# A trunk of an SSD layer and a stick-breaking attention layer: the order of an MLP's last sums, of the first units' projection steps and of the output projection's end

## The chip, the cores and the metric

The kernel runs on one core of one Trainium2 chip. The metric is the device time of one execution in microseconds (us). The kernel before takes 1426.51 us in the median of three runs, from 1426.31 to 1427.24.

The core has five engines with a queue of instructions each. TensorE (PE) multiplies matrices, VectorE (DVE) and ScalarE (ACT) work element by element, GpSimd (POOL) does the small rest, and SyncE (SP) issues the transfers (DMA) of weights. An engine executes its own queue in order. An instruction that waits for another engine holds up all that is queued behind it.

## The reference

A sequence of 512 tokens with 1024 features passes two layers, each of a mixer and an MLP. Each of the four parts ends in `h = LayerNorm(alpha * h + part(h))`. Cut to what the change touches:

```python
# layer 0: Mamba-2 mixer, then
h = layer_norm(ALPHA * h + square(relu(h @ w1)) @ w2)     # first MLP, w1: 1024 x 4096
k, v = h @ w_k, h @ w_v                                   # 16 heads of 64
# layer 1: stick-breaking attention
q = (h @ w_q) * 64 ** -0.5
for each block of 128 queries, key blocks from the diagonal one backwards:
    z = q @ k.T                      # masked: only keys s < t
    # w[t, s] = sigmoid(z[t, s]) * prod over s < j < t of (1 - sigmoid(z[t, j]))
    o += w @ v
h = layer_norm(ALPHA * h + o @ w_o)                       # output projection
h = layer_norm(ALPHA * h + square(relu(h @ w1)) @ w2)     # second MLP
```

## The kernel before

**Numbers in two halves.** Every fp32 operand of a matmul is split into a high part `hi` (rounded to the type fp32r) and a low part `lo`, which is what rounding left out. A product takes three matmuls, hi·hi, hi·lo and lo·hi (`mm3`, lines 207 to 209 of the profile). The high part is a cast on ScalarE (line 190 for weights, 398 for activations), the low part a subtraction on VectorE (192 and 399; every fourth weight tile's on GpSimd in some stretches).

**Weights.** All weight tiles stand in one list, `stream`, in the order in which they are used. `emit_w` fetches the next one by DMA into a raw tile of 128x1024 (line 166), casts it (190) and subtracts (192). `prefetch(n)` does so until n tiles are ready beyond those taken, and `load_w` takes one tile and prefetches some ahead. What is called where in the program decides where a fetch, a cast and a split stand in the queues of SyncE, ScalarE and VectorE. Tiles are numbered along the list: `wr153` is the raw tile, `wh153` and `wl153` its halves. A few tiles go into other buffers (`alt`): `wvp` in the space of the attention's v weights, `wq` and `wk` in that of its q and k weights.

**Order.** A scheduler puts each engine's instructions in order by its own estimate of when they can start, within what the program's order and dependences allow. `tc.issue_after(x)` holds the instructions under it behind instruction x on x's engine; it adds no wait for another engine.

**End of the first MLP.** The second matrix product of an MLP is done in a form with fewer products: seven named ones (P1 to P7) accumulate in banks X, Y, Z and V of PSUM, and `add` (line 431 where the row sums for the norm are taken along) adds a bank to v, the running sum with the residual. A tile of v has four row blocks of 128 tokens. They are normed in pairs, 0 and 1 first, then 2 and 3. `Norm` takes row sums (342), squares (345 on ScalarE), a power on GpSimd (347 to 353), shifts (358) and scales (364) on VectorE; `turn` transposes the normed rows on TensorE (395) and splits them into `ln1_hh` and `ln1_hl` (398, 399), the input of all projections behind. In the last quarter of the first MLP the last two products (P2 into bank V, P3 into Y), their sums and the second pair's norm are all held behind the first pair's norm by one `issue_after`.

**Attention.** The v, q and k projections of head pair 0 (`pv`, `pq`, `pk`) come first. Then a software pipeline runs over 48 units: head pair m (0 to 7), head hd (0, 1), block of queries and keys b (0 to 2). At step s, `z_stage` (lines 1077 to 1096) computes the logits z of unit s and its log terms `sp` (halves `sp..h`, `sp..l`, by ScalarE's Exp and Ln and VectorE's max); `w_stage` (1119 to 1127) of unit s-2 adds the sums over keys on TensorE and takes the exponent, `w..h` and `w..l`; `pv_stage` (1139 to 1153) of unit s-3 multiplies with v into `o`, and after a head's last unit evacuates it (1147 to 1153). A unit is named by its three digits: `w710h` is the high part of w for head pair 7, head 1, block 0. Between the stages `fill.run(step)` puts projection steps of the next head pairs as filler (three matmuls each), 16 or 24 of them over 18 calls. In the last units the output projection's first column half is the filler (`ao`, `ao_early`, `w_o`), as far as head pairs 0 to 5 go.

**Output projection's end and the second MLP's start.** `ao_late` finishes the projection (banks `al`, first digit the column half n, second the row block): for rows 0 and 1 and then rows 2 and 3, what is left of column half 0 (head pairs 6 and 7) and all of half 1, then adds them to v (1040, 1042), takes statistics (1043) and norms. The transposes of rows 0 and 1 stand among the products of rows 2 and 3. `mlp_first` then multiplies the normed rows by the first four weight tiles (bank `f`); two of these tiles are fetched ahead by `ao_late`.

Of the kernel before, what the change touches and what calls it, by code (L numbers as in the profile page):

```python
# [14 lines left out]
ALU = mybir.AluOpType  # L15
PSUM = bass.MemoryType.PSUM

P = 128
T = 512
# [10 lines left out]
ALPHA = (2 * 2) ** 0.25  # L30
# [5 lines left out]
def trunk(ctx: ExitStack, tc: tile.TileContext, io):  # L36
    nc = tc.nc
# [7 lines left out]
    def psum(tag, shape, name):  # L45
        return ps.tile(shape, F32, tag=tag, name=name, bufs=4)
# [32 lines left out]
    ntri_ge = cp.tile([P, P], F32R, name="ntri_ge")  # L79
# [4 lines left out]
    stream = []  # L84
    marks = []
# [13 lines left out]
    def w1_tile(layer, i):  # L99
        return io["w1"][layer, 8 * (i // 8) + M_ORDER[i % 8]]  # L100
# [30 lines left out]
    for m in range(KD - 1):  # L131
        stream += [io["w_qk"][m + 1, j] for j in range(2)]
        if m in v_at:
            stream += [io["w_v"][v_at.index(m) + 1, j] for j in range(2)]
    alt_o = len(stream) + 3
    stream += [io["w_o"][0, i] for i in range(4)] + [w1_tile(1, 0)]
    stream += [io["w_o"][1, i] for i in range(4)] + [w1_tile(1, 1)]
    marks.append(len(stream))
    mlp_stream(1)
    del stream[marks[2]:marks[2] + 2]  # L140
# [1 line left out]
    ready = []  # L142
    taken = [0]
    extra = [None, 0, 0, True, 0]
    alt = {}
    sums = {}
    depth = [2]

# [73 lines left out]
    class Filler:  # L222
# [4 lines left out]
        def add(self, gen):  # L227
            self.queue.append(gen)
# [172 lines left out]
    PAIRS = [(0, 1), (2, 3)]  # L401
# [11 lines left out]
    def mlp(layer, ln, nxt, pts):  # L413
# [5 lines left out]
        with tc.tile_pool(name=f"mlp{layer}", bufs=1, reuse_waits="tile") as mp:  # L419
# [3 lines left out]
            def add(row, n, pts, stats=False, js=(0, 1)):  # L423
                for j in js:
                    t = rows[row][j]
                    vs = v[:, t, n * T:(n + 1) * T]
                    if (t, n) not in started:
                        started.add((t, n))
                        nc.vector.scalar_tensor_tensor(vs, vs, ALPHA, pts[j], ALU.mult, ALU.add)
                    elif stats:  # L430
                        nc.vector.scalar_tensor_tensor(vs, vs, 1.0, pts[j], ALU.mult, ALU.add,
                                                       accum_out=nxt.sm[:, t, n:n + 1])
                    else:
                        nc.vector.tensor_add(vs, pts[j], vs)

            for q in range(4):
                last = q == 3
# [509 lines left out]
    def attention(ln, nxt):  # L947
# [4 lines left out]
        with tc.tile_pool(name="att", bufs=2, reuse_waits="tile") as at:  # L952
# [16 lines left out]
            def qk_w(i):  # L969
                return tuple(at.tile([P, 1024], F32R, tag=n + "2", name=f"w{n}{i}", bufs=2) for n in "qk")  # L970
# [54 lines left out]
            def ao(*args):  # L1025
                for _ in ao_steps(*args):
                    pass
# [8 lines left out]
            def ao_evac(pts, n, tt):  # L1036
                for j, t in enumerate(tt):
# [61 lines left out]
            def w_stage(u):  # L1099
                m, hd, b = u  # L1100
                nm = f"{m}{hd}{b}"
                z, s = st[u]
                n = z.shape[1]
                sa, sb = st[m, hd, 0][1], st[m, hd, min(b, 1)][1]
                off = 0
                for j in blocks[b]:
                    zj = z[:, off:off + qn[j]]
                    own = [x[:, off:off + qn[j]] for x in s]
                    off += qn[j]
                    terms = []  # L1110
                    if j == 2:
                        terms = [(P, [x[:, 2 * P:3 * P] for x in sa])]
                    elif j < 2:
                        terms = [((2 - j) * P, [x.rearrange("p (a c) -> p a c", c=P)[:, 0::3, :] for x in sa])]
                    if j == 0:
                        terms.append((P, sb))
                    for c0, tt in terms:
                        for x in tt:
                            nc.tensor.matmul(zj[:, c0:], none_r, x, start=False, stop=False, skip_group_check=True)
                    for i, x in enumerate(own):  # L1120
                        nc.tensor.matmul(zj, ntri_ge, x, start=False, stop=i == 1, skip_group_check=True)
# [4 lines left out]
                nc.scalar.activation(ws[0], z, AF.Exp)  # L1126
                nc.vector.tensor_sub(ws[1], w, f(ws[0]))
                st[u] = (z, s, ws)
# [36 lines left out]
            w_o, wv_of, w_1, pin = {}, {}, [], [None]  # L1165
# [16 lines left out]
            for s in range(len(units) + 3):  # L1182
                if s < len(units):
# [96 lines left out]
```

## Time and profile before

| what | value |
|---|---|
| median of three runs | 1426.51 us (1426.31 to 1427.24) |
| profiled execution | 1426.79 us |
| span of the profiled execution | 1424.7 us, 19323 instructions |
| matmuls | 7414 |
| DMA | 162.99 MB, 114 GB/s in the mean |

The span runs from the first to the last instruction that the profile shows; 2.1 us of the profiled execution lie around it. The busy share of an engine is a mean over stages with different limits. So a stage is read by itself: in a timeline each row is a start, a duration, the engine, the line, the operation, out<-in, and in brackets how long the engine sat idle before the row and which engine's result ended that wait. PEclk is the clock granted to TensorE, 1.00 being full speed. The chain of waits follows the work that ended last, step by step.

### The profile page before, as it was taken

How to read it: one execution, taken by the hardware profiler on the slowest of the kernel's cores; microseconds unless marked ns; L12 is line 12 of the kernel's file. 1: busy time of each engine (PE TensorE's matmuls, PEld its weight loads, DVE VectorE, ACT ScalarE, POOL GpSimd, SP SyncE). 2: the span in 40 equal slices, each digit the busy share in tenths (PEclk: the TensorE clock that was granted, in tenths of full speed). 3: DMA queues.
4: the chain of work that ended last, by engine and by line, in shares of the span. 5: the costliest groups of instructions: out<-in, count | busy, mean ns of one | idle time of the engine just before them, and what ended most of it. 6: DMA issues, size and time to landing. Idle time of an engine off the chain costs nothing. (4 is left out here: it accounts for less than half of the span.)

```text
span 1424.7 us, 19323 instructions
## 1 busy us (share of the span) xinstructions
PE 1394.1 (98%) x7414; PEld 1199.9 (84%) x7414; DVE 1078.2 (76%) x1530; ACT 783.9 (55%) x1264; POOL 221.4 (16%) x249
## 2 busy tenths in 40 slices
PE   9999999999999999999999899999999999999996
PEld 6898897889997988888888789899878888888885
DVE  5798898368877695876849868787867876858587
ACT  5556574246653453626345468898842735454453
POOL 2344555135443100000000200000000000000001
PEclk9999999999999999999999999999999999999999
DMA  5223212221223356455443421121223455454533
GB/s 185 75 77 131 75 60 75 89 89 60 75 75 104 125 157 179 132 179 161 148 148 120 146 89 38 52 75 45 89 75 118 131 165 162 149 175 136 176 111 126
DMA packets 46699, 162.99 MB, mean 114 GB/s; under 512 B 5520, under 2 KB 5776, under 8 KB 46608
## 3 DMA queue, kind: packets, MB, share of 16 engines
q1 hardware_dynamic: 44016, 157.44, 35.4%
q10 hardware_dynamic: 2592, 4.33, 1.0%
q8 instruction: 58, 0.95, 0.3%
q14 instruction: 33, 0.27, 0.1%
HBM read 159.65 MB, written 2.10 MB: 114 GB/s over the span
## 5 line engine op out<-in xcount | busy, mean ns | idle before, releaser
L190 ACT CAST wh<-wr 128x1024 fp32r<-128x1024 f32 x235 | 246.7, 1050 | 328.5 <-DMA wr<-w 165.1
L192 DVE TENSOR_TENSOR wl<-wr,wh 128x1024 fp32r<-128x1024 f32 x218 | 268.4, 1232 | 184.3 <-ACT wh L190 182.9
L208 PE MATMUL f<-ln_hl,wh 128*128 128x512 f32 (+1 forms) x544 | 201.2, 371 | 0.0
L209 PE MATMUL f<-ln_hh,wl 128*128 128x512 f32 (+1 forms) x544 | 201.1, 370 | 0.0
L207 PE MATMUL f<-ln_hh,wh 128*128 128x512 f32 (+1 forms) x544 | 200.4, 371 | 0.0
L208 PEld LDWEIGHTS f<-ln_hl,wh 128*128 128x128 f32 x544 | 102.3, 188 | 17.6 <-DVE ln_hl L399 0.2
L209 PEld LDWEIGHTS f<-ln_hh,wl 128*128 128x128 f32 x544 | 102.3, 188 | 17.4
L207 PEld LDWEIGHTS f<-ln_hh,wh 128*128 128x128 f32 x544 | 101.9, 188 | 17.5
L347 POOL TENSOR_TENSOR ln_rs<-ln_sums 128x1 f32<-128x1 f32 (+1 forms) x6 | 3.1, 523 | 635.3 <-ACT lnr L345 635.3
L208 PE MATMUL X<-wl,hP 128*128 128x512 f32 x192 | 74.7, 389 | 0.0
L207 PE MATMUL X<-wh,hP 128*128 128x512 f32 x192 | 74.7, 389 | 0.0
L209 PE MATMUL X<-wh,l 128*128 128x512 f32 x192 | 74.2, 390 | 0.2 <-DVE l L460 0.2
L209 PE MATMUL pz<-wh,x_l 128*128 128x256 f32 x256 | 72.8, 284 | 0.0
L208 PE MATMUL pz<-wl,x_h 128*128 128x256 f32 x256 | 72.6, 284 | 0.0
L207 PE MATMUL pz<-wh,x_h 128*128 128x256 f32 x256 | 72.5, 283 | 0.0
L459 ACT CAST hP<-r 128x512 fp32r<-128x512 f32 x80 | 48.1, 620 | 32.4 <-DVE r L471 31.5
L192 POOL TENSOR_TENSOR wl<-wr,wh 128x1024 fp32r<-128x1024 f32 x17 | 42.5, 2503 | 93.3 <-ACT wh L190 92.9
L207 PE MATMUL px<-x_h,wh 128*128 128x512 f32 x128 | 50.8, 397 | 0.0
L208 PE MATMUL px<-x_l,wh 128*128 128x512 f32 x128 | 50.2, 393 | 0.0
L209 PE MATMUL px<-x_h,wl 128*128 128x512 f32 x128 | 50.2, 392 | 0.0
L208 PE MATMUL Y<-wl,hP 128*128 128x512 f32 x128 | 49.8, 389 | 0.0
L208 PEld LDWEIGHTS pz<-wl,x_h 128*128 128x128 f32 x256 | 48.7, 190 | 0.9
(1365 smaller groups left out, 3930.7 us busy)
## 6 DMA issues: line engine op xcount, KB each, us to landing
wr<-w SPq DMA_DIRECT2D x160, 512.0 KB, 3.6
wr<-w_bc SPq DMA_DIRECT2D x16, 512.0 KB, 3.6
wr<-w_x SPq DMA_DIRECT2D x16, 512.0 KB, 3.6
wr<-w_z SPq DMA_DIRECT2D x16, 512.0 KB, 3.5
wr<-w_so SPq DMA_DIRECT2D x16, 512.0 KB, 3.6
rawa<-w SPq DMA_DIRECT2D x16, 512.0 KB, 3.6
rawc<-w SPq DMA_DIRECT2D x16, 512.0 KB, 4.5
wr<-w_qk SPq DMA_DIRECT2D x16, 512.0 KB, 3.6
```

The lines of the kernel that those rows point to most:

```text
L190: nc.scalar.copy(hi, raw)
L192: eng.tensor_sub(lo, raw, f(hi))
L207: nc.tensor.matmul(out, a[0], b[0], start=start, stop=False, skip_group_check=skip)
L208: nc.tensor.matmul(out, a[0], b[1], start=False, stop=False, skip_group_check=skip)
L209: return nc.tensor.matmul(out, a[1], b[0], start=False, stop=stop, skip_group_check=skip)
L347: nc.gpsimd.tensor_add(rs, self.sq[:, t0:t1, 0], self.sq[:, t0:t1, 1])
L459: nc.scalar.copy(h, src)
```

## The change

Three places are changed.

1. **End of the first MLP.** `prefetch` stops at an upper limit (`upto`), which is set to one tile beyond the MLP's own while the last sums are queued and is lifted behind them; then three tiles are prefetched. The sums of bank V are no longer held behind the first pair's norm.
2. **First units.** The first filler call at steps 0 and 1 takes five projection steps more.
3. **Output projection.** The second column half begins earlier: its head pairs 0 and 1 at the last unit's step, its head pair 2 and column half 0's head pair 6 behind the last `w_stage`. The list of weights is rearranged to suit (the tile `w_o[1, 0]` ahead of `w_o[0, 3]`, the second MLP's two first tiles at the end), with the special buffers for other tiles.

```diff
-    alt_o = len(stream) + 3
-    stream += [io["w_o"][0, i] for i in range(4)] + [w1_tile(1, 0)]
-    stream += [io["w_o"][1, i] for i in range(4)] + [w1_tile(1, 1)]
+    alt_o = len(stream) + 4
+    stream += [io["w_o"][0, i] for i in range(3)] + [io["w_o"][1, 0], io["w_o"][0, 3]]
+    stream += [io["w_o"][1, i] for i in range(1, 4)] + [w1_tile(1, i) for i in range(2)]
...
+    upto = [len(stream)]
...
-        while len(ready) < min(len(stream), taken[0] + n):
+        while len(ready) < min(upto[0], taken[0] + n):
...
                 if last and not nxt.final:
                     nxt(rows[2])
+                    upto[0] = marks[1] + 1
                     with tc.issue_after(nxt.end.ins):
                         product("P2", Z)
-                        add(1, 0, Z, True)
+                    add(1, 0, Z, True)
+                    with tc.issue_after(nxt.end.ins):
                         product("P3", Y, False, mid=lambda: nxt.turn(rows[2]))
-                        add(1, 1, Y, True)
+                        end = add(1, 1, Y, True)
+                    upto[0] = len(stream)
+                    with tc.issue_after(end.ins):
+                        prefetch(3)
+                    with tc.issue_after(nxt.end.ins):
                         nxt(rows[1])
                         nxt.turn(rows[1])
                     continue
...
+            def ao_between(s):
+                tt, at_ = PAIRS[0], pin[0]
+                if s == len(units) - 1:
+                    early[1] = banks(1, tt)
+                    with tc.issue_after(at_):
+                        for j, t in enumerate(tt):
+                            ao(early[1][j:j + 1], 1, (t,), (0, 1), 0, 7)
+                elif s == len(units) + 1:
+                    early[0] = banks(0, tt)
+                    with tc.issue_after(w_end[0]):
+                        ao(early[0], 0, tt, (6,), 6, 7)
+                        ao(early[1], 1, tt, (2,), 0, 7)
+                pin[0] = at_
+
             def ao_late(tt, turn):
-                p0, p1 = ([psum(("mm", "bg")[n], [P, T], f"al{n}{t}") for t in tt] for n in range(2))
-                if turn is None:
-                    units_end = pin[0]
-                    ao(p0, 0, tt, (6,), 6, 7)
-                    w_1.append(load_w(w1_tile(1, 0)))
-                    pin[0] = units_end
+                p0, p1 = (early[n] if turn is None else banks(n, tt) for n in range(2))
                 with tc.issue_after(pin[0]):
                     if turn is None:
-                        ao(p1, 1, tt, range(7), 0, 7)
+                        ao(p1, 1, tt, range(3, 7), 0, 7)
+                        w_1.extend(load_w(w1_tile(1, i)) for i in range(2))
                         ao(p0, 0, tt, (7,), 6, 7)
...
                         ao(p1, 1, tt, range(7), 0, 7)
-                        w_1.append(load_w(w1_tile(1, 1)))
                         nxt.turn(turn)
...
-            alt[alt_o + 1] = alt[alt_o + 6] = lambda i: qk_w(i)
+            alt[alt_o + 4] = alt[alt_o + 5] = lambda i: qk_w(i)
...
-                fill.run(step)
+                fill.run(step + (5.0 if s < 2 else 0.0))
...
-            fill.drain()
+                if s >= len(units) - 1:
+                    fill.drain()
+                    ao_between(s)
```

In `w_stage` the last matmul is also kept as `w_end[0]`, and `add` returns its last sum; `banks` allocates the two `al` banks of a column half as before. Lines of the changed kernel are 1 higher from `emit_w` on, 8 higher at the projection's sums (1040 becomes 1048) and 20 or 21 higher in the stages of the units (1119 becomes 1139, 1139 becomes 1160).

The order of the queues shows what the scheduler makes of it. On VectorE at the end of the first MLP, before (the number after a name's last underscore tells buffers apart; `V030` and `Y030` are the banks of products, `ln1_sums` the norm's row sums, `lnr` its weights):

```order
L358 SCALAR_TENSOR_TENSOR v_2507<-v_2507,ln1_sums_111,lnr0_7308 128x1024 x2
L364 SCALAR_TENSOR_TENSOR v_2507<-v_2507,ln1_rs_110,lnr0_7308 128x1024 x2
L192 TENSOR_TENSOR wl152_7409<-wr152_7406,wh152_7408 128x1024
L431 SCALAR_TENSOR_TENSOR v_2507,ln1_sums_111<-v_2507,V030_7391 128x512
L431 SCALAR_TENSOR_TENSOR v_2507,ln1_sums_111<-v_2507,V031_7392 128x512
L192 TENSOR_TENSOR wl153_7427<-wr153_7424,wh153_7426 128x1024
L431 SCALAR_TENSOR_TENSOR v_2507,ln1_sums_111<-v_2507,Y030_7226 128x512
L431 SCALAR_TENSOR_TENSOR v_2507,ln1_sums_111<-v_2507,Y031_7227 128x512
L399 TENSOR_TENSOR ln1_hl_7469<-ln1_b00_7470,ln1_hh_7468 128x2x256
```

And there in the changed kernel:

```order
L359 SCALAR_TENSOR_TENSOR v_2507<-v_2507,ln1_sums_111,lnr0_7308 128x1024
L432 SCALAR_TENSOR_TENSOR v_2507,ln1_sums_111<-v_2507,V030_7391 128x512
L432 SCALAR_TENSOR_TENSOR v_2507,ln1_sums_111<-v_2507,V031_7392 128x512
L359 SCALAR_TENSOR_TENSOR v_2507<-v_2507,ln1_sums_111,lnr0_7308 128x1024
L365 SCALAR_TENSOR_TENSOR v_2507<-v_2507,ln1_rs_110,lnr0_7308 128x1024 x2
L193 TENSOR_TENSOR wl152_7409<-wr152_7406,wh152_7408 128x1024
L432 SCALAR_TENSOR_TENSOR v_2507,ln1_sums_111<-v_2507,Y030_7226 128x512
L432 SCALAR_TENSOR_TENSOR v_2507,ln1_sums_111<-v_2507,Y031_7227 128x512
L193 TENSOR_TENSOR wl153_7497<-wr153_7494,wh153_7496 128x1024
L400 TENSOR_TENSOR ln1_hl_7451<-ln1_b00_7452,ln1_hh_7450 128x2x256
```

V's two sums moved in between the first pair's two shifts, and the split of tile 153 moved from ahead of Y's sums to behind them, ahead of the first low half of the normed rows.

On TensorE at the product of unit 000's w with v, before (`pk1` is a projection of head pair 1, `z000` and `z001` the logits of the first units):

```order
L208 MATMUL pk1_7889<-ln1_hl_7469,wh157_7582 128x512
L209 MATMUL pk1_7889<-ln1_hh_7468,wl157_7583 128x512
L1119 MATMUL z000_7803<-sp000h_7815,none_r_102 128x128
L1119 MATMUL z001_7838<-sp000h_7815,none_r_102 128x256
...
L1121 MATMUL z001_7838<-sp001h_7847,ntri_ge_104 128x384
L1121 MATMUL z001_7838<-sp001l_7848,ntri_ge_104 128x384
L1139 MATMUL o00_7949<-w000h_7904,vp0_7573 128x256
```

And there in the changed kernel (`pv10` is the v projection for head pairs 2 and 3):

```order
L1141 MATMUL z001_7867<-sp001l_7877,ntri_ge_104 128x384
L208 MATMUL pv10_7919<-wh159_7859,ln1_hh_7450 128x256
L209 MATMUL pv10_7919<-wl159_7860,ln1_hh_7450 128x256
L210 MATMUL pv10_7919<-wh159_7859,ln1_hl_7451 128x256
L1139 MATMUL z002_7932<-sp000h_7815,none_r_102 128x256
L1139 MATMUL z002_7932<-sp000l_7816,none_r_102 128x256
L1139 MATMUL z002_7932<-sp001h_7876,none_r_102 128x384
L1160 MATMUL o00_8023<-w000h_7962,vp0_7567 128x256
```

Steps of `pv10` now stand between unit 001's last sums and the product with w000h, where the one followed the other before.

On TensorE in the last units, before (`vp3` is v of head pairs 6 and 7, `o_h` and `o_l` the attention's output):

```order
L1139 MATMUL o70_10048<-w702h_10080,vp3_9219 128x512
L1139 MATMUL o70_10048<-w702l_10081,vp3_9219 128x512
L1139 MATMUL o71_10148<-w710h_10120,vp3_9219 128x256
L207 MATMUL al00_10201<-wvp179_9962,o_h_8226 128x512
L208 MATMUL al00_10201<-wvp179_9962,o_h_8226 128x512
L209 MATMUL al00_10201<-wvp179_9962,o_l_8227 128x512
...
L1139 MATMUL o71_10148<-w710l_10121,vp3_9219 128x256
```

And there in the changed kernel:

```order
L1160 MATMUL o70_10048<-w702h_10080,vp3_9219 128x512
L208 MATMUL al10_10158<-wh179_9962,o_h_8226 128x512
L209 MATMUL al10_10158<-wl179_9963,o_h_8226 128x512
L210 MATMUL al10_10158<-wh179_9962,o_l_8227 128x512
...
L1160 MATMUL o70_10048<-w702l_10081,vp3_9219 128x512
L208 MATMUL al11_10159<-wh179_9962,o_h_8226 128x512
L209 MATMUL al11_10159<-wl179_9963,o_h_8226 128x512
L210 MATMUL al11_10159<-wh179_9962,o_l_8227 128x512
...
L1160 MATMUL o71_10188<-w710h_10120,vp3_9219 128x256
```

Twelve matmuls of column half 1 (six of al10, six of al11) moved between the two products of w702 and in front of that of w710h; before, six of column half 0 stood behind the latter's first matmul.

More of the change, by code (lines that the diff above doesn't have):

```diff
@@ L428, in add @@
                         started.add((t, n))
-                        nc.vector.scalar_tensor_tensor(vs, vs, ALPHA, pts[j], ALU.mult, ALU.add)
+                        end = nc.vector.scalar_tensor_tensor(vs, vs, ALPHA, pts[j], ALU.mult, ALU.add)
                     elif stats:
-                        nc.vector.scalar_tensor_tensor(vs, vs, 1.0, pts[j], ALU.mult, ALU.add,
-                                                       accum_out=nxt.sm[:, t, n:n + 1])
-                    else:
-                        nc.vector.tensor_add(vs, pts[j], vs)
+                        end = nc.vector.scalar_tensor_tensor(vs, vs, 1.0, pts[j], ALU.mult, ALU.add,
+                                                             accum_out=nxt.sm[:, t, n:n + 1])
+                    else:
+                        end = nc.vector.tensor_add(vs, pts[j], vs)
+                return end
             for q in range(4):
@@ L1043, in ao_evac, with banks @@
                     nc.vector.bn_stats(nxt.st[:, t, n, :], vs)
-            def ao_late(tt, turn):
-                p0, p1 = ([psum(("mm", "bg")[n], [P, T], f"al{n}{t}") for t in tt] for n in range(2))
-                if turn is None:
-                    units_end = pin[0]
-                    ao(p0, 0, tt, (6,), 6, 7)
-                    w_1.append(load_w(w1_tile(1, 0)))
-                    pin[0] = units_end
+            def banks(n, tt):
+                return [psum(("mm", "bg")[n], [P, T], f"al{n}{t}") for t in tt]
+            def ao_between(s):
[11 more added lines that the diff above has]
+                pin[0] = at_
+            def ao_late(tt, turn):
+                p0, p1 = (early[n] if turn is None else banks(n, tt) for n in range(2))
                 with tc.issue_after(pin[0]):
                     if turn is None:
-                        ao(p1, 1, tt, range(7), 0, 7)
+                        ao(p1, 1, tt, range(3, 7), 0, 7)
+                        w_1.extend(load_w(w1_tile(1, i)) for i in range(2))
                         ao(p0, 0, tt, (7,), 6, 7)
@@ L1120, in w_stage @@
                     for i, x in enumerate(own):
-                        nc.tensor.matmul(zj, ntri_ge, x, start=False, stop=i == 1, skip_group_check=True)
+                        w_end[0] = nc.tensor.matmul(zj, ntri_ge, x, start=False, stop=i == 1,
+                                                    skip_group_check=True).ins
                 w = at.tile([P, T], F32, tag="wf", name=f"wf{nm}", bufs=2)[:, :n]
@@ L1164, in attention @@
                 nc.gpsimd.memset(f(x[0:64, 1, :]), 0.0)
-            w_o, wv_of, w_1, pin = {}, {}, [], [None]
+            w_o, wv_of, w_1, pin, w_end, early = {}, {}, [], [None], [None], {}
             alt[alt_o] = lambda i: vp_w(i)
-            alt[alt_o + 1] = alt[alt_o + 6] = lambda i: qk_w(i)
+            alt[alt_o + 4] = alt[alt_o + 5] = lambda i: qk_w(i)
             wv = v_alloc(0)
```

## The prediction

> **What bounds the kernel now.** I read the page's busy line first.
>
> ```profile
> PE 1394.1 (98%) x7414; PEld 1199.9 (84%) x7414; DVE 1078.2 (76%) x1530; ACT 783.9 (55%) x1264; POOL 221.4 (16%) x249
> ```
>
> TensorE is busy 1394.1 of 1424.7 us; no other engine is near that. The matmuls stay the same in number and shape, so a change of order can win only where TensorE waits or runs at a lower clock: 30.6 us of idle time, plus what half clock costs. So the next view is that of 5 us windows over the places where the change moves something. Three of them hold much less than 5 us of matmuls:
>
> ```profile
> core 0: us, PE busy (x) PEld busy (x) DVE busy (x) ACT busy (x) POOL busy (x), PEclk, DMA share, GB/s
> 800.00:805.00 5.00, 1.82 (x10) 1.13 (x10) 5.00 (x9) 1.07 (x2) 2.49 (x4) 0.84 0.27 79
> 845.00:850.00 5.00, 3.21 (x17) 2.10 (x15) 4.51 (x8) 4.53 (x10) 0.46 (x1) 1.00 0.00 0
> 1045.00:1050.00 5.00, 3.51 (x18) 2.49 (x17) 4.41 (x7) 3.85 (x9) 0.00 (x0) 1.00 0.60 198
> ```
>
> In all three VectorE is full or nearly so (5.00, 4.51, 4.41) while TensorE waits: there its queue, or ScalarE's at 845, is the bound. The clock column (PEclk) is below 1.00 in the first of them, so I cut 3.4 us windows on the points at which the spacing of matmuls changes:
>
> ```profile
> 800.00:803.40 3.40, 1.82 (x10) 1.00 0.00 0
> 803.40:806.80 3.40, 1.34 (x7) 0.50 0.76 198
> 806.80:810.20 3.40, 3.40 (x17) 0.50 0.29 116
> 847.80:851.20 3.40, 2.27 (x16) 1.00 0.30 80
> 1049.20:1052.60 3.40, 1.64 (x7) 1.00 0.13 42
> 1052.60:1056.00 3.40, 3.40 (x8) 0.50 0.54 181
> 1080.80:1084.20 3.40, 2.60 (x21) 1.00 0.64 161
> ```
>
> Behind each window stand TensorE's busy time, its granted clock and the DMA share. A window with 1.64 or 1.82 us of work is followed by one at half clock, 2.27 and 2.60 are not, and a full one ends it. I put the threshold at about 2 us and use it below. [...]
>
> The price of work at full clock comes from the chain of waits, where neighbours start 0.12 (256 columns) and 0.23 us (512) apart:
>
> ```profile
> 1108.86 0.12 PE f L209
> 1108.98 0.23 PE f L207
> ```
>
> **Part 1, end of the first MLP (about 795 to 820).** The timeline's VectorE rows:
>
> ```profile
> 796.56 1.31 DVE L358 SCALAR_TENSOR_TENSOR v<-v,ln_sums,lnr 128x1024 f32<-128x1024 f32 x1 [0.97 <-ACT lnr L345]
> ...
> 798.74 2.49 DVE L364 SCALAR_TENSOR_TENSOR v<-v,ln_rs,lnr 128x1024 f32<-128x1024 f32 x2 [0.86 <-POOL ln_rs L353]
> ...
> 802.37 0.67 DVE L431 SCALAR_TENSOR_TENSOR v<-v,V 128x512 f32<-128x512 f32 x1
> ...
> 803.59 1.21 DVE L192 TENSOR_TENSOR wl<-wr,wh 128x1024 fp32r<-128x1024 f32 x1
> 804.73 0.67 DVE L431 SCALAR_TENSOR_TENSOR v<-v,Y 128x512 f32<-128x512 f32 x1
> ...
> 805.94 1.28 DVE L399 TENSOR_TENSOR ln_hl<-ln_b,ln_hh 128x512 fp32r<-128x512 f32 x2
> ...
> 805.46 1.97 PE L395 MATMUL ln_b<-ident,v 128*128 128x128 f32 x8 [2.46 <-DVE v L431]
> 807.08 0.56 PE L209 MATMUL pv<-wh,ln_hl 128*128 128x256 f32 x1
> ```
>
> V's two sums (802.37 to 803.59, 1.22 us) move in between the norm's two shifts, where 0.97 and 0.86 us of idle time take them: the scaling at 798.74 doesn't move. If that cover were gone they would cost their 1.22. The split behind them (803.59 to 804.73, 1.14) goes behind Y's sums. So Y's sums start at 802.37, 2.36 earlier, and with them the transposes that waited 2.46 for them. But the displaced split now stands ahead of the first low half of the norm (ln_hl). That one starts behind Y's sums (1.21, as 804.73 to 805.94) and the split (1.14), at 804.72, and is done 0.7 later, near 805.4, in place of 806.6; the matmul that used it at 807.08 starts at 805.5: **1.6 gained**. The half clock then ends about a window's part sooner, since work at 803.4 to 806.8 rises from 1.34 by the 0.6 that the earlier start allows at half speed; I take 0.6 (by where the window's edge falls, +2.4 or −0.8). Against it, ten matmuls that stood between the second pair's transposes and their first user now stand ahead of them; ten times 0.12 is 1.2 of cover lost, of which about half is needed: −0.5. Sum **+1.7**, bounds 0.3 (1.6 − 0.8 − 0.5) and 3.5 (1.6 + 2.4 − 0.5).
>
> **Part 2, the first units (845 to 851).** Steps of the projections stand among units 0 and 1 now.
>
> ```profile
> 846.75 0.49 PE L1119 MATMUL z<-sp000h,none_r 128*128 128x128 f32 x2 [0.34 <-DVE sp000h L1095]
> 847.62 0.33 PE L1119 MATMUL z<-sp000l,none_r 128*128 128x128 f32 x1 [0.37 <-DVE sp000l L1096]
> 850.05 0.39 PE L1139 MATMUL o<-w000h,vp 128*128 128x256 f32 x1 [1.13 <-ACT w000h L1126]
> ```
>
> The three waits are 1.84, and drains around them some 0.5. The extra steps are five per call, three matmuls of 0.12 to 0.23 each: 1.8 to 3.4 us per unit, more than any one wait, and the rows of the order show them ahead of each of the three. I take **+2.0**, with bounds 0.8 (only the first two vanish) and 2.3 (all). The steps are not new, they are taken from later; what then lacks there is a rival below.
>
> **Part 3, the last units (1045 to 1059).** The stretch runs from the product of w702h to the 25th matmul of the output projection's end:
>
> ```profile
> 1045.10 0.39 PE L1139 MATMUL o<-w702h,vp 128*128 128x512 f32 x1
> 1046.40 0.39 PE L1139 MATMUL o<-w710h,vp 128*128 128x256 f32 x1 [0.67 <-ACT w710h L1126]
> 1049.68 0.38 PE L1119 MATMUL z<-sp710h,none_r 128*128 128x256 f32 x1 [0.82 <-DVE u L1090]
> 1052.54 0.78 PE L1139 MATMUL o<-w712h,vp 128*128 128x512 f32 x1 [1.18 <-ACT w712h L1126]
> 1058.97 0.39 PE L207 MATMUL al<-wh,o_h 128*128 128x512 f32 x1
> ...
> 1041.42 1.22 DVE L192 TENSOR_TENSOR wl<-wr,wh 128x1024 fp32r<-128x1024 f32 x1
> 1050.12 0.69 DVE L1096 TENSOR_TENSOR sp712l<-u,sp712h 128x512 fp32r<-128x512 f32 x1
> ...
> 1077.23 3.55 DMA wr<-w
> ```
>
> Its 13.87 us hold 24 projection matmuls (5.5) and unit matmuls of 5888 columns, 11.5 times 0.23 (2.7): 8.2 of work, 5.7 lost (waits of 0.67, 0.82 and 1.18, pipeline drains around them, and 1.7 by the halved window at 1052.6). After the change six projection matmuls (1.4) stand behind the product of w702h, six more behind w702l, and w_o[0,3]'s and w_o[1,1]'s behind unit 712's last sums. The first wait falls whole. The second doesn't: the cast for the next weights stands ahead of unit 712's logarithm on ScalarE and a split (1.22) ahead of its maximum on VectorE, so sp712l ends near 1051.7, where it was 1050.8. I replay 0.95 there and 0.45 for each of the two waits behind it, 1.9 in all, and no halved window, as work in each 3.4 us comes to over 2. So 5.7 − 1.9 = 3.8 would be gained. The DMA for the displaced weight tile is issued behind the split that begins at 1041.42, at 1042.6; with a duration like the 3.55 in the last row (of the chain of waits) it lands at 1046.2, by my replay 0.8 before its cast; what a later landing has beyond that, VectorE and unit 712 are late.
>
> **Part 4, what of it reaches the second MLP (1062 to 1086).** There VectorE's chain decides:
>
> ```profile
> 1065.29 1.37 DVE L1040 TENSOR_TENSOR v<-al,v 128x512 f32<-128x512 f32 x2 [8.52 <-PE al L209]
> 1084.41 0.39 PE L208 MATMUL f<-ln_hl,wq 128*128 128x256 f32 x1 [0.79 <-DVE ln_hl L399]
> ```
>
> It begins at the last product of al00 and al01 (1065.29) and ends in the low half that TensorE waits for at 1084.41. The order puts the six matmuls of column half 1 ahead of that product, relative to before: 1.4 later. So 3.8 − 1.4 = **+2.4** passes; bounds 1.4 (waits in part 3 of 2.9 in place of 1.9) and 3.0 (of 1.3). TensorE is early by the 1.4 that the chain isn't, and idles more: 2.60 us of work in the window at 1080.8 becomes about 1.2, below the threshold, and a half clock is likely. A whole halved window costs 1.7 as at 1052.6, but some of the window is idle anyhow; I take **−1.0**, bounds 0 (none) and −2.5 (it lasts half a window more).
>
> **Sum:** 1.7 + 2.0 + 2.4 − 1.0 = 5.1 us. The profiled execution took 1426.79 and would take 1421.7; the median of the runs is 1426.51, and less 5.1 it is **1421.4**.
>
> **The rivals.**
> 1. *No half clock in part 4.* The idle time might fall in two windows, each above 2 us. Then the sum is 6.1: 1420.4. [...] Against it: 1.2 is far below 1.64. Chance 0.20. [...]
> 2. *Half clock costs more.* It stays for all of 2.5 at part 4 and isn't eased in part 1 (+0.3): 0.3 + 2.0 + 2.4 − 2.5 = 2.2, so 1424.3. Chance 0.13.
> 3. *Part 3 is lost in the queues.* The weight tile lands late, or unit 712's maximum waits longer still: the 2.4 is gone, TensorE isn't early in part 4 either, and sp712l's 0.9 (1051.7 in place of 1050.8) is lost: 1.7 + 2.0 − 0.9 = 2.8, so 1423.7. Chance 0.08.
> 4. *Slower: steps spent early are missing later.* The queue of projection steps then runs dry in later units of the first two heads' pairs, and waits like the 1.13 at 850.05 come back there: at five units 5.7, and two halved windows 3.4, 9.1 in all against part 2's 2.0. Then 5.1 − 2.0 − 9.1 = −6.0: 1432.5. With three such waits and one halved window (5.1) the whole gain is gone; that is the point. Against it: the next projection's (pq2) steps follow directly in the order. Chance 0.06.
> 5. *It doesn't do what it says:* the waits just move to the next instruction; 1426.5. Chance 0.03.
>
> **How the numbers follow.** The forecast holds 0.50; its own range is 1420.4 to 1422.9, since the ends of its terms won't all fall on one side. The range reaches to rival 2's 1424.3 above, and below to 1418.6 (part 1 at its 3.5 and no half clock: 5.1 + 1.8 + 1.0 = 7.9). It leaves out rivals 4 and 5 (0.09) and the tails. A measurement of this kernel tells about 0.2% from nothing, 2.85 us, so faster means below 1423.66: the forecast and rival 1, 0.70, and a small part of rivals 2 and 3, 0.04. Their rest and rival 5 are the same: 0.20. Slower is rival 4: 0.06.
>
> **What would show it.** Part 1: Y's sums near 802.4, transposes right behind, and the pv matmul with the first low half near 805.5. Part 2: no wait over 0.3 at unit 000's product of w. Part 3: the wait for w710h gone, no clock of 0.50 near 1053, sp712l later relative to w702h. Part 4: VectorE's wait for al shorter than 8.52, and a clock of 0.50 near 1085. I would be wrong if new waits for ScalarE or DMA stood in units of the first two head pairs, if the norm's scaling began later by V's sums, or if the clock were low where it was full.

## The result and the profile after

The changed kernel takes **1416.55 us** in the median of four runs (1415.94 to 1419.36), against 1426.59 us before (four runs). The ratio is 0.9934, 95% interval 0.9921 to 0.9946. The gain is 10.0 us; 5.1 were forecast, with a range from 1418.6 to 1424.3. The direction was right and the size half of what came. Two slow executions are left out below: one of `sums_only` (2316.26 us, at a granted clock of 0.555) and one of the kernel before that was timed beside it (3583.47 us).

The page of the changed kernel (span 1414.2 us), its busy line:

```profile
PE 1389.0 (98%) x7414; PEld 1197.0 (85%) x7414; DVE 1076.8 (76%) x1530; ACT 783.8 (55%) x1264; POOL 221.8 (16%) x249
```

TensorE has 5.1 us less of busy time for the same 7414 matmuls. A part of this is clock: the three windows at half clock that the prediction shows hold 1.34, 3.40 and 3.40 us of busy time, 8.1 in all, and half of that, 4.1, would go at full clock. The idle time (1414.2 less 1389.0) is 25.2 us, where it was 30.6: 5.4 less.

To see where the rest went I take five matmuls ahead of which both kernels have issued the same matmuls, so that the time between two of them holds the same work. From the timeline, TensorE alone, of the kernel before:

```profile
799.53 0.39 PE L209 MATMUL Y<-wh,lP 128*128 128x512 f32 x1
...
931.21 0.27 PE L1139 MATMUL o<-w300h,vp 128*128 128x256 f32 x1
...
1080.51 0.40 PE L209 MATMUL al<-wh,o_l 128*128 128x512 f32 x1
...
1130.60 0.39 PE L207 MATMUL X<-wh,hP 128*128 128x512 f32 x1
```

and of the changed kernel (1045.10 of the prediction's rows is the fifth place before):

```profile
798.93 0.40 PE L210 MATMUL Y<-wh,lP 128*128 128x512 f32 x1
...
924.61 0.27 PE L1160 MATMUL o<-w300h,vp 128*128 128x256 f32 x1
...
1038.28 0.39 PE L1160 MATMUL o<-w702h,vp 128*128 128x512 f32 x1
...
1069.64 0.39 PE L210 MATMUL al<-wh,o_l 128*128 128x512 f32 x1
...
1120.11 0.39 PE L208 MATMUL X<-wh,hP 128*128 128x512 f32 x1
```

| stretch | before, us | after, us | difference | forecast |
|---|---|---|---|---|
| start to the first MLP's last Y product | 799.53 | 798.93 | -0.60 | 0 |
| to unit 300's first product with v (parts 1 and 2) | 131.68 | 125.68 | -6.00 | -3.7 |
| to unit 702's product | 113.89 | 113.67 | -0.22 | 0 |
| to the last `al` product (part 3) | 35.41 | 31.36 | -4.05 | -3.8 |
| to the second MLP's first X product (part 4) | 50.09 | 50.47 | +0.38 | +2.4 |
| to the end of the span | 294.1 | 294.1 | 0.0 | 0 |

The 0.60 ahead of the changed code is a difference between two executions: the profile of `changed_again`, the same kernel once more, has this Y product at 800.14, 0.61 later than before. Part 3 came as worked out. Parts 1 and 2 gave 2.3 more, and part 4 took 2.0 less than forecast: these two are what the prediction missed.

Windows of 3.41 us of the changed kernel, cut where the clock's own changes in its trace put their edges (TensorE's busy time, its granted clock, DMA):

```profile
799.37:802.78 3.41, 2.25 (x15) 1.00 0.16 23
802.78:806.19 3.41, 2.33 (x18) 1.00 0.72 227
1069.02:1072.43 3.41, 2.13 (x14) 1.00 0.68 234
```

All three hold more than the 2 us or so at which the prediction put the limit, between its windows of 1.82 and 2.27, and the granted clock is 1.00 from 4.06 to 1406.94 us. Before, it was 0.50 from 803.41 to 810.24 and from 1052.59 to 1056.00. These changes lie on one grid: from the first record of the clock, at 4.70 us of before, they come 234, 2, 71 and 1 times 3.413 us after each other, and the changed kernel's two, at 4.06 and 1406.94, are 411 times 3.413 apart.

### The profile page after: what moved, and what is told of

Its sections match the earlier page's. It is cut to its first block, busy times and chain, and to the rows that moved or that the text cites. A ratio compares the mean times of both kernels' runs of the same rounds, so it can differ in the third digit from the quotient of the medians.

```text
span 1414.2 us, 19327 instructions
## 1 busy us (share of the span) xinstructions
PE 1389.0 (98%) x7414; PEld 1197.0 (85%) x7414; DVE 1076.8 (76%) x1530; ACT 783.8 (55%) x1264; POOL 221.8 (16%) x249
## 4 chain that ended last, share of the span: by engine, by line
PE 87%; DVE 7%; ACT 2%; DMA 2%; issue 1%; POOL 1%; ACTq 0%; SPq 0%; DVEq 0%; POOLq 0%
PE f L209 8%; PE f L210 8%; PE f L208 8%; PE X L210 3%; PE X L208 3%; PE X L209 3%; PE pz L208 2%; PE pz L210 2%; PE pz L209 2%; PE px L208 2%; PE px L209 2%; PE px L210 2%; PE Y L210 2%; PE Y L209 2%; PE Y L208 2%; PE z L1141 1%
```

## The experiments

Theory H: a good part of the gain is the clock. By it a window of 3.41 us in which TensorE has less than about 2 us of work is followed by half clock, as those of 1.82 and 1.64 us were before and the one of 2.27 wasn't, and the change lifts the windows above that. Theory W, the rival, is the prediction's sizing: waits, and the clock as a small correction. Twelve runs were made, one of them the changed kernel once more, each timed beside the kernel before. They are from three chips, on which the kernel before took 1427.15, 1426.71 and 1426.68 us, so times of different chips are compared here with some 0.5 of doubt; the length of a stretch within a trace is the sharper measure.

| run | median, us | ratio to before (95%) |
|---|---|---|
| sums_only | 1424.07 | 0.9978 (0.9969 to 0.9987) |
| steps_only | 1422.92 | 0.9973 (0.9962 to 0.9985) |
| proj_only | 1422.72 | 0.9968 (0.9956 to 0.9981) |
| split_back | 1418.43 | 0.9941 (0.9928 to 0.9955) |
| changed_again | 1417.00 | 0.9937 (0.9924 to 0.9949) |
| two_more_stats | 1422.59 | 0.9964 (0.9951 to 0.9976) |
| low_half_first | 1417.01 | 0.9934 (0.9922 to 0.9947) |
| ten_steps | 1421.74 | 0.9967 (0.9955 to 0.9979) |
| warm_transposes | 1416.78 | 0.9933 (0.9919 to 0.9946) |
| late_casts | 1416.07 | 0.9924 (0.9911 to 0.9936) |
| late_casts_low_half | 1416.29 | 0.9928 (0.9916 to 0.9941) |
| two_and_half_steps | 1418.14 | 0.9938 (0.9925 to 0.9950) |

### Each part alone

`sums_only` is the kernel before with the change's edits in the first MLP alone:

```diff
+                    upto[0] = marks[1] + 1
                     with tc.issue_after(nxt.end.ins):
                         product("P2", Z)
-                        add(1, 0, Z, True)
+                    add(1, 0, Z, True)
```

(with the lifting of the limit behind Y's sums, as in the change).

> The kernel before with part 1 alone (V's sums and the limit on prefetch). Theory H (work per 3.4 us window decides half clock; windows with 1.82 us of work or less are followed by half clock, 2.04 or more are not): the two half-clock windows at the end of the first MLP go too, so 0.8 of order and 2.4 of clock, 3.2 in all: near 1423.4, no clock of 0.50 between 795 and 815. Rival W (the prediction's sizing, waits alone with a slightly shorter half clock): 1.7, near 1424.9, with a clock of 0.50 still there.

`steps_only` has the five steps alone:

```diff
-                fill.run(step)
+                fill.run(step + (5.0 if s < 2 else 0.0))
```

> The kernel before with part 2 alone (five more projection steps at steps 0 and 1). By the trace of the changed kernel the time lost on TensorE between unit 000's start and unit 012 falls by 2.7 to 3.0: near 1423.8. Rival: 2.0 as predicted, or less because part of the 2.7 belongs to the earlier sums: 1424.6 or above.

`proj_only` is the changed kernel with these two undone.

> The kernel before with part 3 alone (the output projection dealt among the last units). By the trace of the changed kernel 3.7 are kept from the last units through the second MLP's start: near 1422.9, and no clock of 0.50 near 1052. Rival (the prediction's sizing of the second MLP's start): 1.4 kept, near 1425.2, with a clock of 0.50 near 1085.

The ratios are 0.22, 0.27 and 0.32% in gain, together 0.81% against 0.66% (0.54 to 0.79%) for the whole: near enough, since each of the four is uncertain by about 0.1, for three gains that add up, with little room for one that lives off another. `proj_only` came where it was expected (1422.72), with no half clock near 1052. `steps_only` (1422.92) has three runs of 1421.10 to 1421.86 at clocks of 0.995 to 0.997 and three of 1423.97 to 1425.71 at 0.992 to 0.994: its kernel still holds both places where the clock can be lost. In the trace the stretches say it more sharply. From the last Y product to unit 300, `sums_only` needs 128.59 us (799.36 to 927.95), 3.09 less than before, and the whole change 6.00 less: 3.1 are part 1's and 2.9 part 2's. From unit 702 to the last `al` product `proj_only` needs 31.33 us, the same 4.08 less as the whole change's 4.05.

Part 1 alone keeps the clock whole at its place, as H says, and leaves it halved at the other. Windows of `sums_only`:

```profile
804.22:807.63 3.41, 2.33 (x19) 1.00 0.75 251
1046.57:1049.98 3.41, 1.92 (x7) 1.00 0.27 88
1049.98:1053.39 3.41, 3.40 (x8) 0.50 0.39 145
```

The median of 1424.07 lies between what the two theories wanted (1423.4 and 1424.9): by itself it doesn't decide.

### Is it the clock?

`split_back` takes the limit on prefetch out of the changed kernel, so that the split of tile 153 stands ahead of Y's sums again:

```diff
-                    upto[0] = marks[1] + 1
```

> The changed kernel without the limit on prefetch: the split of tile 153 stands ahead of Y's sums again, V's sums stay early. The first low half of the normed rows comes no later by this (the same four operations stand ahead of it on VectorE), but the transposes that wait for Y's sums come 1.1 later and leave the first of two 3.4 us windows with about 0.7 less work, 2.25 less 0.7 = 1.5. Theory H: half clock returns, 1.7 to 2.4 slower than the changed kernel: 1418.2 to 1419.0. Theory W (waits alone): no change, 1416.5.

It measured 1418.43, 1.4 to 1.9 slower than the two sets of runs of the changed kernel; but the kernel before was 0.4 to 0.6 slower on this chip too, and against it the difference is 1.0 to 1.3, short of H's 1.7. The trace decides: from the last Y product to unit 300's first product with v `split_back` takes 127.41 us (799.31 to 926.72), where the changed kernel takes 125.68 and `changed_again` 125.58, so 1.7 to 1.8 more, as H has it, and the stretches behind are the same up to 0.2. Unit 300's product and windows of `split_back` and, behind them, its VectorE rows:

```profile
926.72 0.27 PE L1159 MATMUL o<-w300h,vp 128*128 128x256 f32 x1
...
801.18:804.59 3.41, 1.73 (x12) 1.00 0.38 112
804.59:808.01 3.42, 3.42 (x18) 0.50 0.60 200
```

```profile
800.86 2.53 DVE L193 TENSOR_TENSOR wl<-wr,wh 128x1024 fp32r<-128x1024 f32 x2
803.32 0.68 DVE L432 SCALAR_TENSOR_TENSOR v<-v,Y 128x512 f32<-128x512 f32 x1
...
804.53 1.28 DVE L400 TENSOR_TENSOR ln_hl<-ln_b,ln_hh 128x512 fp32r<-128x512 f32 x2
```

From the first split to the first low half are 3.67 us (800.86 to 804.53). In the changed kernel it is 3.58:

```profile
800.12 1.30 DVE L193 TENSOR_TENSOR wl<-wr,wh 128x1024 fp32r<-128x1024 f32 x1
801.35 0.67 DVE L432 SCALAR_TENSOR_TENSOR v<-v,Y 128x512 f32<-128x512 f32 x1
...
802.56 1.21 DVE L193 TENSOR_TENSOR wl<-wr,wh 128x1024 fp32r<-128x1024 f32 x1
803.70 0.68 DVE L400 TENSOR_TENSOR ln_hl<-ln_b,ln_hh 128x512 fp32r<-128x512 f32 x1
```

So what TensorE finally waits for comes at almost the same time; what differs is that the transposes behind Y's sums fall out of a window, and half of the next window's 3.42 us, 1.7, is lost.

`warm_transposes` is `split_back` with eight transposes done twice. They stand where TensorE idles:

```diff
-                for j in range(2):
+                for j in [0, 1] * (2 if self.idx == 1 and t0 == 0 and mm < 2 else 1):
                     m = 2 * mm + j
```

> The kernel of the run split_back (changed kernel without the limit on prefetch, 1418.4) with the eight transposes of the first pair's first two banks done twice, into the same place: eight matmuls of 128 columns, about 0.9 us, more work for TensorE in the time in which it waits for VectorE. Theory H: the window there rises from 1.4 to 1.7 us above 2, the half clock stays away and the kernel gets 1 to 2 us FASTER by more work: 1416.5 to 1417.5, at clocks of 0.997. Theory W: 1418.4, or up to 0.9 slower.

It measured 1416.78: 1.65 us faster than `split_back`, by doing more. About 0.5 of that can be the chip's (the kernel before took 1426.68 us beside it and 1427.15 beside `split_back`). In the trace the stretch to unit 300 takes 126.16 us (798.83 to 924.99), 1.25 less than in `split_back`. Unit 300's product and the windows:

```profile
924.99 0.27 PE L1159 MATMUL o<-w300h,vp 128*128 128x256 f32 x1
...
799.38:802.79 3.41, 2.47 (x18) 1.00 0.11 12
802.79:806.20 3.41, 2.68 (x20) 1.00 0.85 265
```

The medians' intervals (0.9919 to 0.9946 and 0.9928 to 0.9955) overlap in most of their width, so the times alone don't show it. But W has no way at all to a shorter stretch here, the clock is whole where it was halved, and four of the five runs lie at 1416.56 to 1416.83, below all five of `split_back` (1418.18 to 1419.92) by more than the chips differ. I take H as shown for this place.

`changed_again` is the changed kernel, run a second time.

> The changed kernel once more. Theory H: its own runs differ by where the 3.4 us windows fall against the idle time at the end of the first MLP, whose least full window (1.88 us by the trace) is near the limit: most runs near 1416.5 at a clock of 0.997, a few 1 to 3 us above it at 0.995 or less. Theory W (the clock plays no part in the gain): times within 1 us of each other and no tie to the clock.

Its five runs were 1416.12, 1416.66, 1417.00 and 1417.78 at granted clocks of 0.997 to 0.998, and 1419.54 at 0.996; the first set had 1419.36 at 0.995 beside three of 0.997 to 0.998 near 1416.4. So one execution in four or five has a mean clock that is lower by 0.001 to 0.003. One window of 3.41 us at half clock takes 0.0012 off the mean over 1414.2 us, so my estimate is a window or two more at half clock. Edges that fall otherwise from execution to execution would fit that: by the trace of the changed kernel the least work in any 3.41 us at the first MLP's end is 1.88 us (801.03 to 804.44), less than the 1.98 that half clock followed in `low_half_first`, and it's below 2 us for a few positions of the edges only. But neither of the two runs at the lower clock was profiled, so where they lost it isn't shown. The mean clock of a run is also a rough witness: the profiles of `steps_only`, `split_back` and `two_and_half_steps` have a window at half clock behind the one near 238 us (2.40 to 2.41 us of work), far from the change, and it costs about 0.1 us there (20.1 us between the same two matmuls near 230 and 250, where the eleven other profiles have 20.0). A spread of 1.7 within the runs at 0.997 to 0.998 remains. The two profiled runs of this kernel (1416.35 and 1417.78) show where such a difference can arise: the same matmul stands at 19.57 us in the first and at 21.09 in the second, so their difference of 1.43 arose at the start, ahead of all that was changed.

### The first units: how many steps

Both kernels are the changed one with another number in `fill.run(step + ...)`, 2.5 and 10.

> The changed kernel with 2.5 more projection steps at steps 0 and 1 in place of five. Five gave 2.8 (waits at units 000 to 012), ten lost 5 again among units 002 to 300. If the gain is cover for fixed waits, half the steps cover some 1.5 of the 2.8: 1418.0. If less would have been enough, 1416.7 or better.

> The changed kernel with ten more projection steps at steps 0 and 1 in place of five. The trace of the changed kernel has about 1.0 us left to lose among units 000 to 012, so at best 0.5 faster, 1416.0. The rival on steps that are missing later: the queue runs dry among the units of the first pair, and waits of 0.3 to 1.1 come back in several: 1418 or more.

With five steps the view of waits shows none for TensorE from 836 to 900, where before it had 1.1, 0.4 and 0.3. With ten it shows, from 836 to 935:

```profile
PE o L1160 <- ACT w200h L1147: 1.6, 1, 1.6
PE o L1160 <- ACT w010h L1147: 0.8, 1, 0.8
PE o L1160 <- ACT w100h L1147: 0.7, 1, 0.7
PE o L1160 <- ACT w000h L1147: 0.4, 1, 0.4
```

That is the prediction's fourth rival, steps spent early that are missing later, and it costs 4.7 us (1421.74 against 1417.00). It exists, but not at the change's number. With 2.5 steps the time came as expected (1418.14), but not for the reason given: the first units are covered as well as with five, and the one wait is 0.6 at w100h, later. From the last Y product to unit 300 it takes 127.15 us, 1.47 more than with five. So the number five isn't only cover; it also decides which units the queue of steps reaches.

### The second MLP's start

`two_more_stats` makes VectorE's chain there longer:

```diff
                     nc.vector.bn_stats(nxt.st[:, t, n, :], vs)
+                    if n == 1 and t in (0, 1):
+                        nc.vector.bn_stats(nxt.st[:, t, n, :], vs)
```

> The changed kernel with the two statistics of the second column half of rows 0 and 1 taken twice (two BN_STATS of 0.60 us more in VectorE's chain at the second MLP's start; the result is the same). If that chain sets the start, 1.2 slower: 1417.7. Theory H adds a half clock, since the least full window there (2.13 us) loses up to 1.2: another 1.0 to 1.7, so 1418.7 to 1419.4. If TensorE had slack there as the prediction had it before the change, nothing: 1416.5.

Two runs, at clocks of 0.998 and 0.997, took 1418.76 and 1419.60; three, at 0.993 to 0.994, took 1422.59 to 1422.78. The edit did more than was meant. From the first sum with `al` (1055.76) to the first low half the chain runs 20.11 us, 2.92 more than the changed kernel's 17.19, since the scheduler also put a third statistics operation (0.6) and a fourth split (1.14) ahead of that low half:

```profile
1074.74 1.20 DVE L193 TENSOR_TENSOR wl<-wr,wh 128x1024 fp32r<-128x1024 f32 x1
1075.87 1.28 DVE L400 TENSOR_TENSOR ln_hl<-ln_b,ln_hh 128x512 fp32r<-128x512 f32 x2
```

The stretch from the last `al` product to the first X product follows with 53.17 us in place of 50.47, 2.70 more at full clock. So the chain sets the start. In the three other runs 3 to 4 us more come with a lower clock. The least work in any 3.41 us of the profiled run is 1.70 us here, so a half clock at this place, as the prediction feared in part 4, would fit; but none of the three was profiled, and where they lost the clock isn't shown.

Two kernels tried to take waits away that were left. `low_half_first` holds the prefetch behind the first low half:

```diff
-                    with tc.issue_after(end.ins):
+                    with tc.issue_after(nxt.first[1]):
                         prefetch(3)
```

(`first` holds the cast and the subtraction of a `turn`'s first bank.)

> The changed kernel with the three prefetched tiles of the first MLP's end held behind the first low half of the normed rows in place of Y's last sum: the split of tile 153 leaves the place ahead of that low half, for which TensorE waited 1.08 us at 804.43. 0.7 to 1.1 faster, 1415.5 to 1415.9, if nothing else stands ahead of it; no gain if the next low half, now behind the split, takes over the wait whole.

No gain. The first low half comes right behind Y's sums (803.99) and the second behind the split (805.85): 1.86 apart, where the changed kernel has 0.72 (803.70 and 804.42). That profiled run also had a window of 1.98 us at 799.72, and half clock behind it. The windows, and the rows of VectorE:

```profile
799.72:803.13 3.41, 1.98 (x12) 1.00 0.00 0
803.13:806.55 3.42, 3.42 (x16) 0.50 0.52 158
...
803.99 0.68 DVE L400 TENSOR_TENSOR ln_hl<-ln_b,ln_hh 128x512 fp32r<-128x512 f32 x1
804.59 1.21 DVE L193 TENSOR_TENSOR wl<-wr,wh 128x1024 fp32r<-128x1024 f32 x1
...
805.85 0.67 DVE L400 TENSOR_TENSOR ln_hl<-ln_b,ln_hh 128x512 fp32r<-128x512 f32 x1
```

`late_casts` does the like at the second MLP's start, for cast and split:

```diff
+            with tc.issue_after(first[0]), tc.issue_after(first[1]):
+                w_1.extend(load_w(w1_tile(1, m)) for m in range(2, M0))
             pts = mlp_first(1, nxt, w_1)
```

> The changed kernel with the next weight tiles' casts and splits at the second MLP's start held behind the first high and low half of its input (in place of ahead of them; TensorE waited 1.28 us for that cast at 1072.29). The first low half comes one split (1.13 us) sooner: 1.0 faster, 1415.7, and the least full window there rises. Rival: the tile that comes later is then waited for instead, no gain.

> The edits of late_casts and of low_half_first together. low_half_first alone gave no gain (1417.01) as the second low half waited in its place; so the same as late_casts within 0.5, with fewer runs at a lower clock.

`late_casts` came to 1416.07, 0.5 to 0.9 below the changed kernel. TensorE's wait for the first high half, 1.28 us after the change, is 0.35. The first row is the changed kernel's, the second that of `late_casts`:

```profile
1072.29 0.51 PE L208 MATMUL f<-ln_hh,wq 128*128 128x256 f32 x2 [1.28 <-ACT ln_hh L399]
...
1072.51 0.50 PE L208 MATMUL f<-ln_hh,wq 128*128 128x256 f32 x2 [0.35 <-ACT ln_hh L399]
```

In the traces the stretch from the last `al` product to the first X product takes 49.45 us, 1.02 less than in the changed kernel, as expected, and 49.45 with the two edits together too. The ratios' intervals (0.9911 to 0.9936 and 0.9924 to 0.9949) overlap, so the gain is shown for this stretch and not for the whole time. The two edits together gave 1416.29.

## Why the prediction was wrong

**Part 1, forecast 1.7, measured 3.1: mis-sized, in the clock.** The step that failed is "The half clock then ends about a window's part sooner ... I take 0.6". The waits came about as worked out: Y's sums start 2.42 us behind the last Y product (798.93 to 801.35), where it was 5.20 (799.53 to 804.73), 2.78 sooner (forecast 2.36); TensorE's longest wait falls from 2.46, for Y's sums, to 1.08, for the low half behind the displaced split:

```profile
804.43 0.39 PE L210 MATMUL pv<-wh,ln_hl 128*128 128x256 f32 x1 [1.08 <-DVE ln_hl L400]
```

The 0.5 that I took off for lost cover wasn't due: behind this row TensorE doesn't wait again up to 836. And I had the limit of about 2 us in hand and applied it to the second window (1.34 at half clock) only. The step left out was the first window with the transposes moved into it: it holds 2.25 us now, and then no half clock starts at all. Both windows' loss, half of 1.34 + 3.40, is 2.4: the upper bound that I had written down and not taken. `split_back` puts the clock's part at 1.7 (127.41 against 125.68 us), nearly three times the 0.6, and together with `warm_transposes` it shows that this is the clock and not the wait.

**Part 2, forecast 2.0, measured 2.9: mis-sized.** All three waits vanished, as the order had it. I counted 1.84 of wait and 0.5 of drains. In the rows that were quoted a wait is counted from the modelled end of the matmul before, and 0.34 of wait at 846.75 stood for a start 0.74 after a matmul of 0.23 (846.01 to 846.75): 0.51 lost. The three cost 0.51, 0.59 and 1.29, and 0.11 more behind each at the restart, 2.7 in all. The upper bound of 2.3 was too low for that reason.

**Part 3, forecast 3.8, measured 4.05: right.** The wait for w710h is gone, and of the others 0.44 and 0.23 are left:

```profile
1042.91 0.38 PE L1139 MATMUL z<-sp710h,none_r 128*128 128x256 f32 x1 [0.44 <-DVE u L1110]
1044.56 0.50 PE L1141 MATMUL z<-sp712l,ntri_ge 128*128 128x512 f32 x1 [0.23 <-DVE sp712l L1116]
```

The 1.7 of half clock in it is less certain than the rest: it was there in the profiled run of before, while in that of `steps_only`, with the same waits, a window of 2.01 us stayed whole:

```profile
1046.61:1050.02 3.41, 2.01 (x7) 1.00 0.46 159
```

There the stretch takes 34.13 us, 1.28 less than before, so the half clock is worth 1.28 here and the order 2.77; an execution of before that keeps its clock at this place gains the less.

**Part 4, forecast a loss of 2.4 (1.4 of chain and 1.0 of clock), measured 0.4: the step failed.** The chain did begin where I had put it: 1055.79 is 17.51 behind unit 702's product, and it was 20.19, 2.7 sooner (forecast 2.4). But I carried its length over from before, and it is shorter. Before:

```profile
1080.86 1.05 ACT L190 CAST wh<-wr 128x1024 fp32r<-128x1024 f32 x1 [4.31 <-DMA wr<-w]
...
1081.94 1.22 DVE L192 TENSOR_TENSOR wl<-wr,wh 128x1024 fp32r<-128x1024 f32 x1 [0.31 <-ACT wh L190]
1083.08 0.69 DVE L1043 BATCH_NORM_STATS2 ln_st<-v 128x6 f32<-128x512 f32 x1
1083.69 0.67 DVE L399 TENSOR_TENSOR ln_hl<-ln_b,ln_hh 128x512 fp32r<-128x512 f32 x1
```

After:

```profile
1055.79 1.29 DVE L1048 TENSOR_TENSOR v<-al,v 128x512 f32<-128x512 f32 x2 [4.80 <-PE al L210]
...
1071.85 1.22 DVE L193 TENSOR_TENSOR wl<-wr,wh 128x1024 fp32r<-128x1024 f32 x1
1072.98 0.69 DVE L400 TENSOR_TENSOR ln_hl<-ln_b,ln_hh 128x512 fp32r<-128x512 f32 x1
```

It ran 18.40 us from 1065.29 to 1083.69, and now 17.19 from 1055.79 to 1072.98. One statistics operation (0.6) went behind the low half, and the split doesn't wait any longer for a cast that waited for a late weight tile. The first could be read from the order of the queues and the second from the rows of before; I took from them the start of the chain and not its members. With the 1.2 the chain wins 3.9 of the 4.05 that TensorE does, TensorE isn't early, its window there holds 2.13 us in place of 1.2, and the half clock stays away. That the chain sets the start is borne out by `late_casts` (a cast and a split less ahead of the first high and low halves, the stretch 1.02 shorter) and by `two_more_stats` (the chain 2.92 longer, the stretch 2.70). That less idle time is what keeps the clock whole is argued from the 2.13 us; no run shows it here.

**The rivals.** The first one (no half clock in part 4) is what happened, for another reason than given: the idle time wasn't split over two windows, there was less of it. The second and third didn't occur. The fourth occurs at ten steps and not at five. How the idle time is split depends on where the windows' edges fall, and that differs from run to run: the edge lies 0.44 us behind the last Y product in the changed kernel, 1.45 in `sums_only` and 1.87 in `split_back` (799.37, 800.81 and 801.18), though the matmuls are the same up to there. And none of the windows ahead of a half clock at the places of the change was empty: they held 1.64 to 1.98 us of work.

## What to carry to other kernels

Where a kernel is bound by TensorE, look at each 3.4 us in which it has only about 2 us of work: at the places of this change a wait there cost itself and, where the window held 1.98 us or less, up to half a window of matmuls behind it (1.7 us), and moving even small work into such a stretch paid (1.25 us in `warm_transposes`). Before carrying a chain's length over to a changed order, list its members again on both sides, the waits for weights among them. Filler that is dealt out early has a best number; both less and more of it were slower here.

## What the runs showed of the hardware

More work made the kernel faster: eight transposes done a second time, 127.41 to 126.16 us in the stretch that they stand in. No limit in the busy time that a profile shows holds everywhere. At the places of the change, windows of 1.98 us (`low_half_first`), 1.92 (`sums_only`), 1.82 and 1.64 (before) and 1.73 (`split_back`) were followed by half clock, and those of 2.01 (`steps_only`) and of 2.13, 2.25 and 2.33 (the changed kernel) at full clock were not. But near 238 us, far from the change, a window of 2.4 us was followed by half clock in three of the fourteen profiled runs, `steps_only`, `split_back` and `two_and_half_steps` (at a cost of about 0.1 us there, against 1.7 at the first MLP's end), and one of 1.50 at the end of `proj_only` was not. What decides it beside the busy time is left open.
